# A causal pool mixer whose window sums are taken by VectorE, against one whose running means are matrix products on TensorE

## The chip, the cores and the metric

One core of one Trainium2 chip runs the whole kernel: TensorE (PE, with its weight loads as PEld), VectorE (DVE), ScalarE (ACT), GpSimd (POOL) and SyncE (SP), which issues most of the loads. The metric is the device time of one launch, in microseconds, as the median over runs.

## The reference

Two transformer blocks over 256 tokens of width 1024. The first block has two layers; the change is in layer 0, whose mixer is this:

```python
def pool_mixer(u, pool_w, pool_scale):                 # u: 256 tokens x 768 = 4 groups of 192
    ...
    win = jnp.array(POOL_WINDOWS, jnp.int32)           # 2, 4, 8, 16
    lo = jnp.maximum(t + 1 - win[None, :], 0)
    cnt = jnp.minimum(t + 1, win[None, :])
    window_sum = csum[:, 1:] - csum[:, lo, ...]
    d = window_sum / cnt - uf                          # mean of the last w tokens, less the own one
    mixed = jnp.einsum('bsgc,gcd->bsgd', d, pool_w)    # one 192 x 192 product for each group
    return mixed.reshape(B, S, MAIN_WIDTH) * pool_scale

proj = rmsnorm(h, norm_mix[l]) @ w_in[l]
main, mq = proj[..., :MAIN_WIDTH], proj[..., MAIN_WIDTH:]
main_out = pool_mixer(main, pool_w[l], pool_scale[l])
mem_out = memory_attention(mqh, mk, mv)                # 4 heads over 256 memory rows
h = h + jnp.concatenate([main_out, mem_out], -1) @ w_out[l]
```

The mean runs over tokens and `pool_w` over channels, so the two may be taken in either order.

## The kernel before

All 256 tokens stay on the chip (two tiles `tt` of 128). Weights stream in as units of 256 rows x 512 columns; ACT casts each to `wh`, DVE makes the rest `wl = raw - wh`, and every large product is three fp32r products (`xh*wh`, `xh*wl`, `xl*wh`) on PE. PE's program is one fixed order of instructions; in the first stage it is written by hand, later a planner (`Line`) lays tasks by rank and estimated lateness, and a scheduler fixes each engine's order. Each engine runs its own queue in order and waits on semaphores.

The part that matters is the first 110 us:

- **In projection, transposed.** Six banks `ups` of channels x tokens (128 x 256) are summed from `w_in` and the raw input; `queries` does the 256 columns of the memory queries into `qs`. The norm of each token, `x_r`, comes later than the products, so it is put in afterwards: `dg` is a diagonal of `x_r`, the products of `ones` with `dg` (L807) spread it over all partitions, `rb` is their copy, and `u = ups * rb` (L817) is the mixer's input.
- **Memory keys and values, layer 0 and 1.** `rows` sums `mem @ w_mem_kv[0]` into `accs1`: 48 fp32r products of 512 columns. `memkv1` follows with 48 more, then the 96 of `out0`.
- **`pool_mix`.** For each of four window levels DVE (tiles 0 to 4) and POOL (tile 5) add shifted copies into `win`, correct the first tokens by `short`, and write `mean - u` back into `u` (L923 to L929). A group of 192 channels lies across two of the six tiles, so the eight `PIECES` are 128 or 64 partitions high. Then 16 fp32 products `mm<-u,pw` with 256 columns follow, whose contraction is 128 or 64 channels and whose output 128 or 64 partitions. ACT (L944) and DVE (L945) split each result to `xh`, `xl` of `mts`, which `out0` reads.
- **`mem_attention`.** Scores `acc<-mkT,mqT` (contraction 64), softmax on DVE and ACT (tile `me`), four transposes `mm<-ident,me` for each half, values `mm<-eT,mv` (64 output partitions).
- **`out0`.** `mixer_out` with no cuts: every row tile is one sum over all eight k-tiles and waits for both `pooled` and `recalled[tt]`.

An fp32 product is run as two passes (two rows in the trace); an fp32r product is one, and so is a transpose.

Of the kernel before, what the change touches and what calls it, by code (L numbers as in the profile page):

```python
# [41 lines left out]
def kernel(  # L42
# [149 lines left out]
    def col(i, n=1):  # L192
        return cols[:, i:i + n]
# [94 lines left out]
    def plan_rows(key, w, cuts):  # L288
        for k0, k1 in zip((0,) + cuts, cuts + (KT,)):
            for c in range(2):  # L290
                planned((key, k0, c), [(w, c * 512, 512)], k1 - k0, k0 * P)
# [2 lines left out]
        planned(("in0", c), [(w_in[0], c * 512, 512)])  # L294
    planned("memkv0", [(w_mem_kv[0], 0, 512)], g=G_MEM + 0)
    planned("memkv1", [(w_mem_kv[1], 0, 512)], g=G_MEM + 8)
    plan_rows("out0", w_out[0], ())
    plan_mlp("mlp0", 8, lambda b: [(w_up[0], b * 512, 512)], w_down[0], 4)
    planned("kv", [(w_kv, 0, 512)], g=G_KV)
    plan_cols("in1", w_in[1], G_MIX + 8)  # L300
# [377 lines left out]

    act.open("mix0", 7)

    u = act.tile([P, 6, S], F32, tag="u", name="u")
    mq = [act.tile([P, 256], F32, tag="mq", name="mq", bufs=TT) for _ in range(TT)]


# [4 lines left out]
    short = act.tile([P, 4, 16], F32, tag="short", name="short")  # L689

    def pool_short():
        cnt = act.tile([P, 16], F32, tag="cnt", name="cnt")
        G.iota(cnt, [[1, 16]], base=1, channel_multiplier=0, allow_small_or_imprecise_dtypes=True)
        V.reciprocal(cnt, cnt)
        for g, w in enumerate(WIN):
            V.tensor_scalar(short[:, g, :], cnt, float(w), None, op0=ALU.mult)

    def run(steps):
        for _ in steps:
# [24 lines left out]
    with tc.manual_schedule(engines={ET.DVE, ET.Activation, ET.Pool, ET.PE}):  # L724

        x_raw, m_raw = raw_T(), raw_T()

        warm = mm_bank()
        for _ in range(12):
            PE.matmul(warm[:, :P], ones, ones, start=True, stop=True)  # L730

        def units_of(i, **a):
            key, w = plan[i][:2]
            ready[key] = []
            units = load_units(*w, **a)

            def more():
                ready[key] += next(units)
                return ready[key][-KU:], len(ready[key]) - KU

            return more

        def columns_T(ps, xs, w, k, c0):

            for i, (wh, wl) in enumerate(w):
                xh, xl = ktiles(xs)[k + i]
                c = slice(c0, c0 + P)
                for j, (a, b) in enumerate(((wh, xh), (wh, xl), (wl, xh))):
                    mm(ps, a[:, c], b, k + i + j == 0, k + i == KT - 1 and j == 2)

        def rows(accs, xs, w, k):
            for tt in range(TT):
                run(lin(accs[tt], ktiles(xs, tt)[k:k + KU], w, k == 0, k + KU == KT))


        load_T(x_raw, xT, 0, 2)
        nc.scalar.dma_start(gcols, gains)
        load_T(x_raw, xT, 2, 2, nc.scalar)

        A.activation(early, ones[:, :1], AF.Copy, scale=2.0)  # L760
        ups = [acc_bank()[:, :S] for _ in range(4)]
        more = units_of(0, apart=KU + 1)
        for k in range(0, KT, KU):
            if k >= 4:
# [7 lines left out]
        pool_short()  # L772
# [12 lines left out]
        dg = act.tile([P, TT, P], F32, tag="dg", name="dg")  # L785
        nx = [Norm(h[tt]) for tt in range(TT)]
        for tt in range(TT):
            for c in range(2):
                nx[tt].add(c)
            x_r[tt] = nx[tt].rstd()  # L790
            V.tensor_scalar(dg[:, tt, :], ident, x_r[tt], None, op0=ALU.mult)
        split_raw(m_raw, mem_set, 0, 4)
        qs = mm_bank().rearrange("p (t c) -> p t c", t=TT)
        rb = act.tile([P, S], F32, tag="rb", name="rb")
        m = [act.tile([P, D], F32, tag="raw_T", name="mem", bufs=4) for _ in range(TT)]
        more = units_of(2)

        def queries(tt):
            run(lin(qs[:, tt, :], ktiles(xs0, tt), [(wh[:, 256:], wl[:, 256:]) for wh, wl in ws]))

        def mem_rows(tt):
            mem_r[tt] = row_norm(m[tt])

        queries(0)
        ps = mm_bank()[:, :S]
        for tt in range(TT):
            PE.matmul(ps[:, tok(tt)], ones, dg[:, tt, :], start=True, stop=True)  # L807
        nc.gpsimd.dma_start(pw, pool_w[0].rearrange("g a d -> (g a) d").rearrange("(j p) d -> p j d", p=P))

        split_raw(m_raw, mem_set, 4, 4)  # L810
        w0 = more()
        tc.keep_in_program_order(nc.sync.dma_start(m[0], mem[0, tok(0), :]))
        mem_rows(0)
        A.copy(rb, ps)
        queries(1)
        for i in range(6):
            V.tensor_tensor(u[:, i, :], ups[i], rb, ALU.mult)  # L817
        w1 = more()
        accs1 = [acc_bank() for _ in range(2)]
        rows(accs1, mem_set, *w0)  # L820
        tc.keep_in_program_order(nc.sync.dma_start(m[1], mem[0, tok(1), :]))
        mem_rows(1)
        rows(accs1, mem_set, *w1)
        for tt in range(TT):
            A.activation(mq[tt], qs[:, tt, :], AF.Copy, scale=x_r[tt])
        for _ in range(2):
            rows(accs1, mem_set, *more())
        for e in mem_there:
            e.at()
    W("memkv0")  # L830
# [80 lines left out]

    def pool_mix(xs, done):

        a, b = (act.tile([P, 6, S], F32, tag="win", name="win", bufs=2) for _ in range(2))
        prev = u
        for lev, (k0, s) in enumerate(((0, a), (1, b), (3, a), (4, b))):
            n = 1 << lev
            for eng, t0, t1 in ((V, k0, 5), (G, 5, 6)):  # L920
                if t0 < t1:
                    o = slice(t0, t1)
                    eng.tensor_copy(s[:, o, :n], prev[:, o, :n])  # L923
                    eng.tensor_tensor(s[:, o, n:], prev[:, o, n:], prev[:, o, :S - n], ALU.add)  # L924
            for k, p0, p1, g in PIECES:
                if g == lev:
                    r, w = s[p0:p1, k, :], WIN[g]
                    V.tensor_tensor(r[:, :w], r[:, :w], short[p0:p1, g, :w], ALU.mult)  # L928
                    V.scalar_tensor_tensor(u[p0:p1, k, :], r, 1.0 / w, u[p0:p1, k, :], op0=ALU.mult, op1=ALU.subtract)  # L929
            prev = s  # L930
        for k0 in range(0, 6, 2):
            yield 6.0 if k0 == 0 else 0
            ps = mm_bank().rearrange("p (k t) -> p k t", t=S)
            for k in (k0, k0 + 1):
                for t, q0, q1, g in PIECES:
                    if t != k:
                        continue
                    d0 = k * P + q0 - g * 192
                    src = [(t2, r0, r1) for t2, r0, r1, g2 in PIECES if g2 == g]
                    for i, (t2, r0, r1) in enumerate(src):  # L940
                        mm(ps[q0:q1, k - k0, :], pw[r0:r1, t2, d0:d0 + q1 - q0], u[r0:r1, t2, :],
                           i == 0, i == len(src) - 1)
                xh, xl = (t[:, k, :] for t in xs)
                A.activation(xh, ps[:, k - k0, :], AF.Copy, scale=col(V_PSCALE + k))  # L944
                V.scalar_tensor_tensor(xl, ps[:, k - k0, :], col(V_PSCALE + k), xh.bitcast(F32),  # L945
                                       op0=ALU.mult, op1=ALU.subtract)
        done.at(1.5)

    mem_kv = {0: add_mem_kv(0, 0, 6.0, accs1)}


# [6 lines left out]
    mts = xset()  # L958
# [3 lines left out]
    line.add(4, pool_mix(mts, pooled))  # L962
# [628 lines left out]
```

## Time and profile before

| | |
|---|---|
| median of 3 runs | 1034.71 us (1034.3 to 1035.31) |
| the profiled execution | 1037.36 us, its span 1035.4 us |
| PE busy | 1027.9 us (99% of the span) |
| DVE, ACT, POOL busy | 638.5, 562.8, 97.7 us |
| mean granted clock of TensorE | 0.997 |

PE is busy almost the whole span, but a row of PE holds about 0.17 us of pipeline beyond the start of the next, so short waits don't show as idle time: the spacing of starts is what to read. The span is that of the profiled execution; 1.96 us of its time lie around it.

### The profile page before, as it was taken

The page shows a single profiled execution, that of the slowest core. Times are in us where ns is not written, and L with a number is a line of the kernel's source. Part 1 is how long each engine was busy: PE and PEld are TensorE (multiplying, and loading weights), DVE is VectorE, ACT ScalarE, POOL GpSimd, SP SyncE. Part 2 cuts the span into 40 slices and gives each one's busy share as a digit, 9 for nine tenths or more (in the row PEclk, how much of TensorE's full clock was granted, in tenths as well). Part 3 has the DMA queues.
Part 4 walks back from the last instruction along what each step waited for, and adds up shares of the span by engine and source line. Part 5 has one row for each costly group of instructions (what it writes and reads, how often), then busy time and mean ns, then how long its engine had stood idle before and what let it go on. Part 6 is the DMA issues. An engine that isn't in the chain of part 4 may idle for free.

```text
span 1035.4 us, 18410 instructions
## 1 busy us (share of the span) xinstructions
PE 1027.9 (99%) x7352; PEld 907.0 (88%) x7352; DVE 638.5 (62%) x1002; ACT 562.8 (54%) x902; POOL 97.7 (9%) x143
## 2 busy tenths in 40 slices
PE   9999999999999999999999999999999999999998
PEld 8858999998876788899988988888999988999997
DVE  6976665555678766564576569847635766464552
ACT  7855554454678654444465445758644556344351
POOL 1515000000143000000001003330000000000000
PEclk9989999999999999999999999999999999999999
DMA  9854556556642259666557554344355566565741
GB/s 341 273 161 138 187 179 211 183 167 208 195 163 82 66 183 322 202 193 211 168 183 246 182 164 157 118 135 149 116 201 186 165 197 209 164 211 163 234 145 41
DMA packets 107765, 186.40 MB, mean 180 GB/s; under 512 B 6808, under 2 KB 31648, under 8 KB 107680
## 3 DMA queue, kind: packets, MB, share of 16 engines
q1 hardware_dynamic: 106160, 180.13, 53.2%
q0 software_dynamic: 1104, 4.80, 1.4%
q8 instruction: 57, 0.93, 0.4%
q10 hardware_dynamic: 416, 0.30, 0.1%
q14 instruction: 28, 0.23, 0.1%
HBM read 182.58 MB, written 2.63 MB: 179 GB/s over the span
## 4 chain that ended last, share of the span: by engine, by line
PE 97%; DVE 1%; DMA 0%; issue 0%; ACT 0%; SPq 0%; ACTq 0%
PE acc L152 61%; PE mm L152 34%; PE mm L159 3%; DMA raw<-in_w_in_dram 0%; DVE wl L243 0%; DVE u L929 0%; DVE wl L248 0%; DVE win L924 0%; DVE win L928 0%; DVE hs L424 0%; ACT wh L242 0%; ACT wh L247 0%; ACT mv L847 0%; SPq L232 0%; PE mm L807 0%
## 5 line engine op out<-in xcount | busy, mean ns | idle before, releaser
L243 DVE TENSOR_TENSOR wl<-raw,wh 128x1024 fp32r<-128x1024 f32 (+1 forms) x316 | 378.1, 1219 | 173.3 <-ACT wh L242 168.0
L242 ACT CAST wh<-raw 128x1024 fp32r<-128x1024 f32 (+1 forms) x316 | 322.5, 1045 | 169.0 <-PE acc L152 100.0
L152 PE MATMUL mm<-xh,wh 128*128 128x256 f32 x752 | 208.3, 277 | 0.0
L152 PE MATMUL mm<-xl,wh 128*128 128x256 f32 x752 | 207.9, 276 | 0.0
L152 PE MATMUL mm<-xh,wl 128*128 128x256 f32 x752 | 207.8, 276 | 0.0
L152 PEld LDWEIGHTS mm<-xh,wh 128*128 128x128 f32 x752 | 141.2, 188 | 1.4 <-issue 0.4
L152 PEld LDWEIGHTS mm<-xl,wh 128*128 128x128 f32 x752 | 141.3, 188 | 1.0
L152 PEld LDWEIGHTS mm<-xh,wl 128*128 128x128 f32 x752 | 141.3, 188 | 0.0
L152 PE MATMUL acc<-wh,xh 128*128 128x512 f32 x336 | 138.6, 412 | 0.0
L152 PE MATMUL acc<-wh,yl 128*128 128x512 f32 x342 | 134.7, 394 | 0.0
L152 PE MATMUL acc<-wl,yh 128*128 128x512 f32 x342 | 134.0, 392 | 0.0
L152 PE MATMUL acc<-wh,yh 128*128 128x512 f32 x342 | 133.4, 390 | 0.0
L152 PE MATMUL acc<-wh,xl 128*128 128x512 f32 x336 | 132.7, 395 | 0.0
L152 PE MATMUL acc<-wl,xh 128*128 128x512 f32 x336 | 132.5, 394 | 0.0
L152 PE MATMUL acc<-xh,wh 128*128 128x256 f32 x416 | 117.0, 281 | 0.5 <-ACT wh L242 0.5
L152 PE MATMUL acc<-xh,wl 128*128 128x256 f32 x416 | 116.5, 280 | 0.4 <-DVE wl L243 0.4
L152 PE MATMUL acc<-xl,wh 128*128 128x256 f32 x416 | 116.3, 279 | 0.0
L152 PEld LDWEIGHTS acc<-xh,wl 128*128 128x128 f32 x416 | 78.8, 189 | 0.9 <-DVE wl L243 0.9
L152 PEld LDWEIGHTS acc<-xh,wh 128*128 128x128 f32 x416 | 78.6, 189 | 0.9 <-ACT wh L242 0.7
L152 PEld LDWEIGHTS acc<-xl,wh 128*128 128x128 f32 x416 | 78.1, 188 | 0.0
L152 PEld LDWEIGHTS acc<-wh,xh 128*128 128x128 f32 x336 | 63.4, 189 | 15.2 <-issue 3.2
L152 PEld LDWEIGHTS acc<-wl,yh 128*128 128x128 f32 x342 | 64.2, 188 | 13.7
(239 smaller groups left out, 1278.7 us busy)
## 6 DMA issues: line engine op xcount, KB each, us to landing
raw<-in_w_in_dram SPq DMA_DIRECT2D x86, 512.0 KB, 4.9
raw<-in_w_up_dram SPq DMA_DIRECT2D x64, 512.0 KB, 4.7
raw<-in_w_down_dram SPq DMA_DIRECT2D x64, 512.0 KB, 4.8
raw<-in_w_out_dram SPq DMA_DIRECT2D x24, 512.0 KB, 4.7
raw<-in_w_ffn_gate_dram SPq DMA_DIRECT2D x44, 256.0 KB, 4.3
raw<-in_w_ffn_up_dram SPq DMA_DIRECT2D x44, 256.0 KB, 4.6
raw<-in_w_ffn_down_dram SPq DMA_DIRECT2D x22, 512.0 KB, 5.1
raw<-in_w_mem_kv_dram SPq DMA_DIRECT2D x8, 512.0 KB, 9.2
```

The costliest lines, as they stand in the source:

```text
L152: PE.matmul(out_, lhsT, rhs, start=start, stop=stop)
L159: PE.transpose(out_, in_, ident)
L242: A.copy(wh[:, ks, :], raw[:, ks, :])
L243: V.tensor_sub(wl[:, ks, :], raw[:, ks, :], wh[:, ks, :].bitcast(F32))
```

## The change

The mixer's order is turned round. `pool_groups(tt)` first multiplies each group's raw channels by `pool_w` (tokens as output partitions, 192 columns), and ACT scales by the token's norm on the way out, to `yp`: so `dg`, `rb` and the products with `ones` are gone, and `u` is a plain copy of `ups`. `pool_mix` then takes the mean less the own token as products with `means`, constant matrices over tokens, made once at the start by POOL and DVE: for each piece 128 columns of tile 0, 128 of tile 1, and 16 that carry tile 0's last tokens into tile 1. The window sums on DVE and POOL are gone. `pool_groups` and `pool_mix` are written into the hand-ordered stage between `rows`, and `out0` is cut into k-tiles 0 to 5 and 6 to 7, so that the first part waits for `pooled` alone.

```diff
-    plan_rows("out0", w_out[0], ())
+    plan_rows("out0", w_out[0], (6,))
...
+    FIRST, OWN = P + 16, P
+    means = act.tile([P, 4, FIRST + OWN], F32, tag="means", name="means")
+    def pool_windows():
...
+        for g, w in enumerate(WIN):
+            G.memset(means[:, g, :], 1.0 / w)
+            V.tensor_scalar(means[:, g, :16], cnt, float(w), None, op0=ALU.min)
+            V.reciprocal(means[:, g, :16], means[:, g, :16])
+        for g, w in enumerate(WIN):
+            for m in (means[:, g, :FIRST], means[:, g, FIRST:]):
+                n = m.shape[1]
+                G.affine_select(m, m, [[1, n]], ALU.is_ge, 0.0, base=0, channel_multiplier=-1)
+                G.affine_select(m, m, [[-1, n]], ALU.is_ge, 0.0, base=w - 1, channel_multiplier=1)
+    def pool_less_own():
+        for m in (means[:, :, :P], means[:, :, FIRST:]):
+            V.tensor_tensor(m, m, ident[:, None, :].to_broadcast([P, 4, P]), ALU.subtract)
...
-            V.tensor_scalar(dg[:, tt, :], ident, x_r[tt], None, op0=ALU.mult)
-            PE.matmul(ps[:, tok(tt)], ones, dg[:, tt, :], start=True, stop=True)
-        A.copy(rb, ps)
-            V.tensor_tensor(u[:, i, :], ups[i], rb, ALU.mult)
+            V.tensor_copy(u[:, i, :], ups[i])
...
+        def pool_groups(tt):
+            for g0 in range(2):
+                ps = mm_bank()[:, :384].rearrange("p (g d) -> p g d", g=2)
+                for g in (g0, g0 + 2):
+                    src = [(t, r0, r1) for t, r0, r1, g2 in PIECES if g2 == g]
+                    for i, (t, r0, r1) in enumerate(src):
+                        mm(ps[:, g // 2, :], u[r0:r1, t, tok(tt)], pw[r0:r1, t, :], i == 0, i == len(src) - 1)
+                A.activation(yp[:, tt]..., ps, AF.Copy, scale=x_r[tt])
+        def pool_mix(xs, k0):
...
+                    mm(o[:, :P], yp[:, 0, f], means[:, g, :P])
+                    mm(o[:, P:], yp[:, 1, f], means[:, g, FIRST:], True, False)
+                    mm(o[:, P:FIRST], yp[:, 0, f], means[:, g, P:FIRST], False, True)
...
-    t = mixer_out("out0", mts, (), [[[pooled, recalled[tt]]] for tt in range(TT)])
+    t = mixer_out("out0", mts, (6,), [[[pooled], [recalled[tt]]] for tt in range(TT)])
```

The order on PE where the mixer's products stand, before: they come as `mm<-u,pw` after all of `memkv1`, among the scores of the memory attention (`mkT`, `mqT`).

```order
L159 MATMUL mm<-ident,ks 128x128 x4
L152 MATMUL mm<-u,pw 128x256 x4
L152 MATMUL acc<-mkT_571,mqT 128x256 x4
L152 MATMUL mm<-u,pw 64x256 x4
L152 MATMUL acc<-mkT_571,mqT 128x256 x2
L152 MATMUL acc<-wh,xh 128x512
...
L152 MATMUL mm<-u,pw 64x256 x4
...
L152 MATMUL mm<-u,pw 128x256 x2
L152 MATMUL acc<-mkT_571,mqT 128x256
L152 MATMUL mm<-u,pw 128x256 x2
```

Now the 16 group products (`mm<-pw,u`, in two lots of 8) stand between the first three units of `memkv0`, and the products with `means` among those of `memkv1`; here the second lot of the latter, k-tiles 3 and 4.

```order
L152 MATMUL acc<-wh,xh 128x512
L152 MATMUL mm<-means,yp 128x128 x2
L152 MATMUL mm<-means,yp 128x16
L152 MATMUL mm<-means,yp 64x128 x2
L152 MATMUL mm<-means,yp 64x16
L152 MATMUL mm<-means,yp 64x128 x2
L152 MATMUL mm<-means,yp 64x16
L159 MATMUL mm<-ident,mq 128x128 x4
L152 MATMUL acc<-wl,xh 128x512
```

So what waited for DVE's window sums late in the stage now waits for ACT's `yp` early in it. The memory attention stands alone afterwards on PE, after `memkv1`, with the first part of `out0` around it; the last two score products are split off behind four products of `memkv1`.

```order
L152 MATMUL acc<-mkT_654,mqT 128x256 x6
L152 MATMUL acc<-wh,xl 128x512
L152 MATMUL acc<-wh,xh 128x512
L152 MATMUL acc<-wl,xh 128x512
L152 MATMUL acc<-wh,xl 128x512
L152 MATMUL acc<-mkT_654,mqT 128x256 x2
L159 MATMUL mm<-ident,me 128x128 x4
L159 MATMUL mm<-ident,ks 128x128 x2
```

Before, its scores and its values were spread over four places each; now the scores stand in two places and the sixteen value products in one.

## Rows read from the trace of the kernel before

**Rows 1.** The page: busy time, clock in 40 slices, chain by engine.

```profile
PE 1027.9 (99%) x7352; PEld 907.0 (88%) x7352; DVE 638.5 (62%) x1002; ACT 562.8 (54%) x902; POOL 97.7 (9%) x143
...
PEclk9989999999999999999999999999999999999999
...
PE 97%; DVE 1%; DMA 0%; issue 0%; ACT 0%; SPq 0%; ACTq 0%
```

**Rows 2.** Stretches: length, each engine's busy time (instructions), granted clock, DMA.

```profile
49.00:55.50 6.50, 5.36 (x27) 2.38 (x25) 6.38 (x17) 3.40 (x7) 1.91 (x1) 1.00 0.31 101
55.50:62.20 6.70, 6.70 (x17) 3.40 (x17) 3.79 (x9) 0.47 (x1) 1.62 (x2) 0.50 0.71 237
```

**Rows 3.** The chain that ended last, in order of time: start, length, work.

```profile
51.27 1.14 DVE wl L243
...
52.63 1.24 DVE wl L243
...
83.12 4.15 PE acc L152 x18
```

**Rows 4.** Timeline of PE, 49 to 67 us: start, length, passes [idle before].

```profile
49.14 1.86 PE L152 MATMUL mm<-u,pw 128*128 128x256 f32 x8
50.93 1.13 PE L152 MATMUL acc<-mkT,mqT 64*128 64x256 f32 x8
52.00 1.22 PE L152 MATMUL mm<-u,pw 128*64 128x256 f32 x4
54.36 1.22 PE L152 MATMUL mm<-u,pw 64*64 64x256 f32 x4 [1.14 <-DVE u L929]
55.51 2.07 PE L152 MATMUL acc<-mkT,mqT 64*128 64x256 f32 x4
...
59.94 2.88 PE L152 MATMUL mm<-u,pw 128*64 128x256 f32 x8
...
63.78 1.00 PE L152 MATMUL mm<-u,pw 128*128 128x256 f32 x3
...
66.07 0.60 PE L159 MATMUL mm<-ident,me 128*128 128x128 f32 x4
```

**Rows 5.** Timeline of PE elsewhere: fp32 passes of few columns.

```profile
27.12 0.61 PE L807 MATMUL mm<-dg,ones 128*128 128x128 f32 x4
...
655.35 1.10 PE L152 MATMUL mm<-fQ,fK 128*32 128x32 f32 x32
...
676.82 2.17 PE L152 MATMUL mm<-hv,AT 128*128 128x128 f32 x18
678.83 0.39 PE L152 MATMUL mm<-hv,AX 128*128 128x128 f32 x2
```

**Rows 6.** Timeline of PE: one of four runs of value products.

```profile
73.93 1.09 PE L152 MATMUL mm<-eT,mv 128*64 128x128 f32 x14
```

**Rows 7.** The load of `pw`: its issue on POOL, and its landing.

```profile
23.52 1.07 POOL L808 DMA_DIRECT2D pw<-in_pool_w_dram  x1
...
DMA to landing us min/median/max: 7.9/7.9/7.9
```

**Rows 8.** Timeline of DVE and ACT: softmax of the memory attention.

```profile
57.40 1.28 DVE L887 TENSOR_REDUCE ms<-acc 128x2 f32<-128x512 f32 x2
...
63.23 0.56 ACT L892 ACTIVATE me<-acc,ms,mr 128x256 f32<-128x256 f32 x1
```

**Rows 9.** Timeline of POOL and DVE: a select, and DVE beside POOL.

```profile
1.19 0.28 POOL L200 TENSOR_SCALAR_AFFINE_SELECT ident<-ones 128x128 f32<-128x128 f32 x1
...
7.07 0.69 DVE L243 TENSOR_TENSOR wl<-raw,wh 128x512 fp32r<-128x512 f32 x1 [0.97 <-ACT wh L242]
...
26.49 1.41 DVE L248 SCALAR_TENSOR_TENSOR wl<-raw,gcols,wh 128x512 fp32r<-128x512 f32 x2
...
38.16 3.27 DVE L248 SCALAR_TENSOR_TENSOR wl<-raw,gcols,wh 128x512 fp32r<-128x512 f32 x4
...
38.85 1.47 POOL L345 TENSOR_TENSOR mr<-hs,mhalf 128x4 f32<-128x4 f32 x1
```

More of the change, by code (lines that the diff above doesn't have):

```diff
@@ L681 @@
     u = act.tile([P, 6, S], F32, tag="u", name="u")
+    yp = act.tile([P, TT, 768], F32, tag="yp", name="yp")
     mq = [act.tile([P, 256], F32, tag="mq", name="mq", bufs=TT) for _ in range(TT)]
@@ L687 @@
               (3, 0, P, 2), (4, 0, 64, 2), (4, 64, P, 3), (5, 0, P, 3))
-    short = act.tile([P, 4, 16], F32, tag="short", name="short")
-    def pool_short():
+    FIRST, OWN = P + 16, P
+    means = act.tile([P, 4, FIRST + OWN], F32, tag="means", name="means")
+    def pool_windows():
         cnt = act.tile([P, 16], F32, tag="cnt", name="cnt")
         G.iota(cnt, [[1, 16]], base=1, channel_multiplier=0, allow_small_or_imprecise_dtypes=True)
-        V.reciprocal(cnt, cnt)
         for g, w in enumerate(WIN):
-            V.tensor_scalar(short[:, g, :], cnt, float(w), None, op0=ALU.mult)
+            G.memset(means[:, g, :], 1.0 / w)
[9 more added lines that the diff above has]
+            V.tensor_tensor(m, m, ident[:, None, :].to_broadcast([P, 4, P]), ALU.subtract)
     def run(steps):
@@ L726 @@
         x_raw, m_raw = raw_T(), raw_T()
+        pool_windows()
         warm = mm_bank()
@@ L771 @@
         more = units_of(1)
-        pool_short()
         ws = []
@@ L783 @@
             load_T(m_raw, memT, k, 4)
-        dg = act.tile([P, TT, P], F32, tag="dg", name="dg")
+        for i in range(6):
+            V.tensor_copy(u[:, i, :], ups[i])
+        pool_less_own()
         nx = [Norm(h[tt]) for tt in range(TT)]
@@ L790 @@
             x_r[tt] = nx[tt].rstd()
-            V.tensor_scalar(dg[:, tt, :], ident, x_r[tt], None, op0=ALU.mult)
+        nc.gpsimd.dma_start(pw, pool_w[0].rearrange("g a d -> (g a) d").rearrange("(j p) d -> p j d", p=P))
         split_raw(m_raw, mem_set, 0, 4)
         qs = mm_bank().rearrange("p (t c) -> p t c", t=TT)
-        rb = act.tile([P, S], F32, tag="rb", name="rb")
         m = [act.tile([P, D], F32, tag="raw_T", name="mem", bufs=4) for _ in range(TT)]
@@ L802, in mem_rows @@
             mem_r[tt] = row_norm(m[tt])
+        def pool_groups(tt):
[5 more added lines that the diff above has]
+                        mm(ps[:, g // 2, :], u[r0:r1, t, tok(tt)], pw[r0:r1, t, :], i == 0, i == len(src) - 1)
+                A.activation(yp[:, tt].rearrange("p (a b d) -> p b a d", a=2, b=2)[:, g0], ps, AF.Copy, scale=x_r[tt])
@@ new lines, in pool_mix @@
+        def pool_mix(xs, k0):
+            ps = mm_bank().rearrange("p (k t) -> p k t", t=S)
+            for k in (k0, k0 + 1):
+                for t, q0, q1, g in PIECES:
+                    if t != k:
+                        continue
+                    o, f = ps[q0:q1, k - k0, :], slice(k * P + q0, k * P + q1)
+                    mm(o[:, :P], yp[:, 0, f], means[:, g, :P])
+                    mm(o[:, P:], yp[:, 1, f], means[:, g, FIRST:], True, False)
+                    mm(o[:, P:FIRST], yp[:, 0, f], means[:, g, P:FIRST], False, True)
+                xh, xl = (t[:, k, :] for t in xs)
+                A.activation(xh, ps[:, k - k0, :], AF.Copy, scale=col(V_PSCALE + k))
+                V.scalar_tensor_tensor(xl, ps[:, k - k0, :], col(V_PSCALE + k), xh.bitcast(F32),
+                                       op0=ALU.mult, op1=ALU.subtract)
@@ L804 @@
         queries(0)
-        ps = mm_bank()[:, :S]
-        for tt in range(TT):
-            PE.matmul(ps[:, tok(tt)], ones, dg[:, tt, :], start=True, stop=True)
-        nc.gpsimd.dma_start(pw, pool_w[0].rearrange("g a d -> (g a) d").rearrange("(j p) d -> p j d", p=P))
+        queries(1)
         split_raw(m_raw, mem_set, 4, 4)
-        w0 = more()
+        w = more()
         tc.keep_in_program_order(nc.sync.dma_start(m[0], mem[0, tok(0), :]))
         mem_rows(0)
-        A.copy(rb, ps)
-        queries(1)
@@ L816 @@
-        for i in range(6):
-            V.tensor_tensor(u[:, i, :], ups[i], rb, ALU.mult)
-        w1 = more()
         accs1 = [acc_bank() for _ in range(2)]
-        rows(accs1, mem_set, *w0)
+        rows(accs1, mem_set, *w)
+        w = more()
         tc.keep_in_program_order(nc.sync.dma_start(m[1], mem[0, tok(1), :]))
-        mem_rows(1)
-        rows(accs1, mem_set, *w1)
         for tt in range(TT):
             A.activation(mq[tt], qs[:, tt, :], AF.Copy, scale=x_r[tt])
-        for _ in range(2):
-            rows(accs1, mem_set, *more())
+        pool_groups(0)
@@ L828 @@
+        mem_rows(1)
+        rows(accs1, mem_set, *w)
+        w = more()
+        pool_groups(1)
+        rows(accs1, mem_set, *w)
+        rows(accs1, mem_set, *more())
+        mts = xset()
+        for k0 in range(0, 6, 2):
+            pool_mix(mts, k0)
         for e in mem_there:
@@ L910, in mem_attention @@
         done.at(3.0)
[L914 to L947, printed above, removed]
     mem_kv = {0: add_mem_kv(0, 0, 6.0, accs1)}
@@ L956 @@
         V.scalar_tensor_tensor(qk_gain[:, i:i + 1], col(a), s, col(b), op0=ALU.mult, op1=ALU.mult)
-    mts = xset()
     mem_kv[1] = add_mem_kv(1, 14, 9.0)
@@ L961 @@
     q_there.at()
-    line.add(4, pool_mix(mts, pooled))
+    pooled.at(2.0)
     for tt in range(TT):
```

## The prediction

> **What bounds the kernel now.** I read the page first: PE is busy for 1027.9 of 1035.4 us and holds 97% of the chain that ended last [rows 1]. So a change here is worth what it adds to PE's own work, plus the few places where PE waits or runs slowly. The clock line has one slice of 40 with an 8, the third, 51.8 to 77.7 us [rows 1]. The table of stretches says what that is: from 55.5 to 62.2 us the granted clock is 0.50, the lower of the two levels (1.2 against 2.4 GHz), and beside it, from 49.0 to 55.5, it is 1.00 [rows 2]. The chain of waits leaves PE just ahead of this: DVE makes two `wl` (51.27, 52.63) and only then the last piece of `u`, and PE's timeline shows the wait for it, 1.14 us before 54.36 [rows 3, 4]. DVE is busy for 6.38 of the 6.50 us there [rows 2]. So the pool mixer costs PE three things: its products, a wait of 1.14 us on DVE, and a slow stretch that begins 1.1 us after that wait.
>
> **What the change removes.** The wait: 1.14 us [rows 4]. The slow stretch: 6.70 us at half the clock, so 3.35 us, if it doesn't come back; what PE did before it fell is the wait and a run of half-height products [rows 2, 4]. Together 4.5 us.
>
> The 32 passes `u,pw`, by starts: 49.14 to 50.93 is 1.79; the four from 52.00, 1.22 less about 0.17 of pipeline, 1.05; 54.36 to 55.51, 1.15; the eight from 59.94 took 2.88, most at half clock (until about 62.3), at full clock 1.6; 63.78 to 66.07 holds the last eight, and two score passes beside them, about 2.2 [rows 4]. Sum 7.8 us. The four passes with `ones`: 18 passes of that size took 676.82 to 678.83, or 0.112 us each, so 0.45 us [rows 5]. Removed in all 4.5 + 7.8 + 0.45 = 12.75 us.
>
> DVE's sums over `win` are off the list: they cost PE the 1.14 us and no more.
>
> **What it adds on PE.** *Group products*: per token tile eight products of 192 columns, 16 passes. Such a pass stands between 0.112 (128 columns) and the 256 columns of the first eight `u,pw`. Those eight lasted 1.79 us, with four of them (contraction 64, on the two halves of the array) side by side: six slots, some 0.22 each, and the rest, about 0.4, is two changes between full and half height, 0.2 each [rows 4, 5]. Midway I take 0.166 a pass. Contraction 128: 4 products x 2 x 0.166 = 1.33; contraction 64: four products, of which two adjacent ones run side by side, 3 x 2 x 0.166 = 1.0; six changes x 0.2 = 1.2. That is 3.5 us, and twice 7.0 us.
>
> *Products with `means`*: eight pieces, each four passes of 128 columns and two of 16. A 16-column pass behind a fresh load of 128 weight columns is nowhere in the trace. Above it stands the 128-column pass, 0.112; below, the passes of 32 columns with 32 weight columns, 32 in 1.10 us, 0.033 each [rows 5]. It loads as many weights as the first, so I take 0.11. Four full-height pieces: 4 x 6 x 0.112 = 2.7. Four half-height ones load 64 columns, so 4 x (4 x 0.112 + 2 x 0.06) = 2.3, less 0.4 where the second of two neighbours starts on the other half before the first has ended. Their four changes: 0.6. Sum 5.2 us.
>
> The Trainium skill (TensorE: Matmul & The Clock Gate, "LDWEIGHTS (loading the stationary operand)") puts a weight load at its columns over 1.2 GHz, whatever the contraction, so 107 ns for 128. By that rule, an estimate from the page, the 16-column passes cost as much as those of 128 and the 5.2 us stand; by the lower row they would be 4.5.
>
> *Order*: the sixteen value products, before in four runs, become one. A run of 14 passes, mostly in pairs, took 1.09 us, 0.75 of it passes [rows 6], so three runs fewer give back about 3 x 0.4 = 1.2 us. The scores lose 0.3 of it: two products of the second token tile fall on one half of the array and can't pair. Net 0.9 us off.
>
> So PE's work: + 7.0 + 5.2 - 7.8 - 0.45 - 0.9 = + 3.05 us.
>
> **New waits.** *Scores.* The last two score products write a bank that the first two filled, so they wait until its maxima and its exponentials have been taken: 1.28 us (two maxima), some 0.2 for the small products, two exponentials of 0.56, 0.1 of signalling, 2.7 us [rows 8]. PE has meanwhile two score products (0.85), four of 512 columns (4.15 / 18 = 0.23 each, 0.92 [rows 3]) and two changes (0.4): 2.2. So it waits 0.5 us. Queued behind are the transposes of `me`, and DVE and ACT feed them no later than PE then comes.
> *Start.* POOL now makes 16 selects of about 0.28 us from 2.5 us on; some ten fall on DVE's first `xl` and `wl`, which PE awaits [rows 9]. DVE beside POOL is slower: two `wl` alone took 1.41 us, four beside POOL 3.27 [rows 9], 0.45 more. Between nothing and ten selects in full (2.8 us, which the stream from 8 us on partly absorbs) I take 0.3.
>
> **Priced at nothing.** The eight small DVE instructions that make `means` stand ahead of the first `xl`, while the first loads are on their way; at 7.07 DVE still waits 0.97 us for ACT [rows 9]. In the stream's way they would cost at most 0.28 us each, the select's time on eight times the columns. Plain copies `u` cost what the products with `rb` did, and move before `wl`, where `queries` (48 passes) cover them. `pw` was issued at 23.52 and landed 7.9 us later, at 31.4 [rows 7]; it was needed at 49.14 and is now needed near 32.7 us (12 products of 0.23 behind the start of `rows` at 29.96, which is 0.45 earlier). One `x` tile now loads ahead of the last three `w_in` units, and they ahead of the norms, so POOL's issue slips by about 0.9 us: cover 0.4 us, and beyond it each 0.1 us late is 0.1 us of PE. ACT's four `yp` stand in front of `wh` units that PE wants only a unit later. The second residual of `out0` (four more DVE additions) lies under 12 products each time.
>
> **The sum.** - 4.5 + 3.05 + 0.5 + 0.3 = - 0.65, call it - 0.7 us. Against the profiled 1037.36 us (span 1035.4 and 1.96 around it) that is 1036.7. The runs shown have a median of 1034.71, 2.65 us below the profiled execution, so the forecast is 1034.0 us.
>
> **The rivals.**
> *Slower: the clock gives nothing back.* Either the timed runs hold no slow stretch (they are 2.65 us faster than the profiled one, and it cost 3.35), or the new wait at the scores brings it on again, as the wait of 1.14 us did at 54.36 [rows 2, 4]. For it: the new wait too stands among half-height passes. Against it: the new wait is half as long, and the three runs lie within 1.0 us of each other, so all of them or none hold the slow stretch, as the profiled one does. The price is 3.35 us: 1037.4 us. It decides from 1.4 us at 0.50 (0.7 lost, no gain left); 5.5 us make it slower by 0.2%.
> *Faster: the small products are cheaper.* If changes cost 0.1 rather than 0.2 (16 of them, 1.6 us) and 16-column passes 0.033 (0.7 us), and the wait at the scores vanishes because maxima and exponentials start before the fourth product is done (0.5): 2.5 to 2.8 us less, 1031.3 us. For it: 32 small passes in 1.10 us [rows 5]; against: all `u,pw` runs show the larger change.
> *DVE is held up at the start.* The Trainium skill (SBUF — State Buffer, "Who interferes with whom") says that a DVE instruction with two SBUF inputs and a GpSimd one that reads SBUF exclude each other for the whole instruction. The trace agrees as far as the 3.27 us go. As a mechanism of this kernel: DVE's `wl` at 7.07, the last that PE waits for at the start, comes behind selects of 0.28 us [rows 9]; four such meetings are 1.1 us in place of 0.3, so 1034.8 us.
>
> **How the numbers follow.** Forecast (within 1.5 us of 1034.0) 0.48; small products cheap 0.24; the clock 0.20; the start 0.08. 0.2% is 2.07 us, about what a measurement of this kernel can tell from none. Faster: the second case and a twelfth of the first, 0.28. Slower: the clock, and a little of the first and last, 0.22. Same: 0.50. The range runs from 1031.3, most of the cheap case, to 1037.4; the likeliest case's own is 1032.5 to 1035.5.
>
> **What would show it.** Right: in the profile after, no idle on PE between 45 and 65 us; 1.00 in every stretch up to 90 us; 32 passes `pw,u` in about 7.0 us and the 48 passes `means,yp` in about 5.2; a wait of about 0.5 us before the last score products; the first `wl` up to 0.3 us later. It would be wrong if 0.50 appears in a stretch again, if PE waits for `pw`, for `yp` or for `wh` in `memkv0`, or if passes at a change cost half of what I took.

## The result: slower by 0.7%

The change takes 1043.2 us (median of 6 runs, 1039.23 to 1044.86), and the kernel before 1035.01 us beside it: a ratio of 1.0071 (95% interval 1.0050 to 1.0093). The forecast was 1034.0 us, and its range ended at 1037.4. The profiled execution of the change took 1044.86 us, its span 1043.2 us.

The page of the change, the lines that answer to [rows 1]:

```profile
PE 1033.2 (99%) x7396; PEld 914.4 (88%) x7396; DVE 635.4 (61%) x985; ACT 564.4 (54%) x905; POOL 98.7 (9%) x155
...
PEclk9899999999999999999999999999999999999999
...
PE 95%; DMA 3%; ACT 1%; issue 0%; DVE 0%; POOL 0%; ACTq 0%; DVEq 0%
```

PE still holds the chain, but loads (DMA) have 3% of it where they had none (`pw` alone 1%), and ACT has 1%. One slice of the clock line holds an 8, as before, but it is now the second. The table of stretches of the change (length, busy time and instructions of PE, PEld, DVE, ACT and POOL, granted clock, DMA share, GB/s) answers to [rows 2]:

```profile
25.00:36.10 11.10, 9.21 (x63) 7.73 (x62) 6.70 (x10) 5.87 (x12) 3.81 (x4) 1.00 1.04 376
36.10:43.00 6.90, 6.90 (x20) 4.82 (x18) 1.20 (x2) 3.60 (x8) 0.86 (x2) 0.51 0.07 25
...
55.50:62.20 6.70, 6.70 (x53) 6.02 (x50) 6.34 (x12) 6.25 (x12) 3.75 (x5) 1.00 0.66 223
62.20:73.60 11.40, 9.55 (x51) 7.24 (x49) 10.00 (x17) 7.62 (x16) 2.31 (x3) 1.00 0.91 280
73.60:80.60 7.00, 7.00 (x23) 5.48 (x24) 3.56 (x14) 4.23 (x15) 0.00 (x0) 0.51 0.17 64
```

The slow stretch of before, at 55.5 us, is gone (1.00). Two others have come, from 36.1 and from 73.6 us, each at half clock. PE's timeline of the change (start, length, passes, idle before) shows what stands ahead of each; it answers to [rows 4]. A row pass is one product of 512 columns (`acc<-wh,xh` and its like), a lot the eight group products of one token tile, which are 16 passes:

```profile
34.27 5.05 PE L152 MATMUL mm<-pw,u 128*128 128x192 f32 x16 [1.89 <-DMA pw<-in_pool_w_dram]
...
39.55 0.63 PE L152 MATMUL acc<-wl,xh 128*128 128x512 f32 x1
39.97 0.63 PE L152 MATMUL acc<-wh,xl 128*128 128x512 f32 x1
...
43.68 3.62 PE L152 MATMUL mm<-pw,u 128*128 128x192 f32 x16
...
68.54 1.99 PE L152 MATMUL acc<-mkT,mqT 64*128 64x256 f32 x12
...
73.52 1.93 PE L152 MATMUL acc<-mkT,mqT 64*128 64x256 f32 x4 [1.85 <-ACT me L933]
```

PE waits 1.89 us for the load of `pw`, and the clock falls 1.9 us later; it waits 1.85 us for the exponentials `me` ahead of the last score products, and the clock falls 0.2 us after that. The first lot of group products takes 5.05 us against 3.62 for the second, and the row passes behind it step by 0.42 instead of 0.23 us. So 3.74 us of waits stand where 1.14 stood, and each slow stretch, some 6.9 us at half the clock, costs about 3.4 us.

Where the first wait comes from: POOL's timeline, with the landing of `pw`, answers to [rows 7], and SP's issues show one load of `h` ahead of the last three of `w_in`.

```profile
24.92 1.07 POOL L807 DMA_DIRECT2D pw<-in_pool_w_dram  x1
...
DMA to landing us min/median/max: 9.2/9.2/9.2
...
6.55 0.60 SPq L795 DMA_DIRECT2D h<-in_x_dram  x1
7.92 5.30 SPq L232 DMA_DIRECT2D raw<-in_w_in_dram  x3
```

SP's issues in the kernel before had the last five loads of `w_in` in a row, and both loads of `h` behind them:

```profile
5.22 8.02 SPq L232 DMA_DIRECT2D raw<-in_w_in_dram  x5
13.29 0.93 SPq L780 DMA_DIRECT2D h<-in_x_dram  x2
```

The load of `pw` is issued 1.40 us later than before and takes 1.3 us longer, so it lands at 34.1 us; PE is there at 34.27 - 1.89 = 32.4. Where the second comes from: DVE's and ACT's timelines around the scores, which answer to [rows 8]:

```profile
68.12 2.78 DVE L243 TENSOR_TENSOR wl<-raw,wh 128x1024 fp32r<-128x1024 f32 x2
70.83 1.27 DVE L928 TENSOR_REDUCE ms<-acc 128x2 f32<-128x512 f32 x2
72.03 0.27 DVE L929 TENSOR_TENSOR ms<-ms,mr 128x2 f32<-128x2 f32 x2
...
72.26 0.56 ACT L933 ACTIVATE me<-acc,ms,mr 128x256 f32<-128x256 f32 x1 [2.95 <-DVE ms L929]
72.82 0.56 ACT L933 ACTIVATE me<-acc,ms,mr 128x256 f32<-128x256 f32 x1
```

The first maximum starts as the second `wl` ends: in DVE's order two copies of later weights stand ahead of it. ACT, which takes the exponentials, sits idle for 2.95 us until DVE's maxima are there.

### The profile page after: what moved, and what is told of

Same layout as the page of the kernel before. It is cut to its first block, busy times and chain, and to the rows that moved or that the text cites. A ratio compares the mean times of both kernels' runs of the same rounds, so it can differ in the third digit from the quotient of the medians.

```text
span 1043.2 us, 18508 instructions
## 1 busy us (share of the span) xinstructions
PE 1033.2 (99%) x7396; PEld 914.4 (88%) x7396; DVE 635.4 (61%) x985; ACT 564.4 (54%) x905; POOL 98.7 (9%) x155
## 4 chain that ended last, share of the span: by engine, by line
PE 95%; DMA 3%; ACT 1%; issue 0%; DVE 0%; POOL 0%; ACTq 0%; DVEq 0%
PE acc L152 59%; PE mm L152 33%; PE mm L159 3%; DMA raw<-in_w_in_dram 1%; DMA pw<-in_pool_w_dram 1%; DMA raw_T<-in_xT_dram 0%; ACT wh L242 0%; ACT xn L395 0%; DVE wl L243 0%; ACT me L933 0%; DVE ms L928 0%; POOL st L345 0%; ACT mv L888 0%; ACTq L773 0%; DVE h L1539 0%
## 5 line engine op out<-in xcount | busy, mean ns | idle before, releaser
L152 PEld LDWEIGHTS acc<-wh,xl 128*128 128x128 f32 x336 | 63.8, 190 | 14.4 <-issue 0.3
```

The source lines that it names most:

```text
L152: PE.matmul(out_, lhsT, rhs, start=start, stop=stop)
```

## The experiments

Theory: the two waits, with the lower clock behind each, are the whole loss, and they come from the late load and from the scores. Rivals: the products themselves cost more than was reckoned; the lower clock belongs to their half-height passes and not to waits; the cut of the output rows is to blame. Every ratio is to the kernel before on the same chip. Waits are those of PE in the profiled run from 0.25 us up; the ones ahead of 9 us (1.05 us for `ones`, the others under 0.7) and near 614 to 626 us (0.5 to 1.4 us, in all but one of the kernels) are left out. The clock is that of the profiled run, with 0.5 for each stretch at half clock (the last 2 us of the span left out). The last column counts the timed runs whose mean granted clock over the whole span was 0.999 or 1.000: a stretch of 6.83 us at half clock takes 0.003 off this mean.

| run | median us | ratio (95%) | waits of PE | granted clock | runs at 0.999 or 1.000 |
|---|---|---|---|---|---|
| the change | 1043.2 | 1.0071 (1.0050 to 1.0093) | 1.89, 1.85 | 0.5 twice | 0 of 6 |
| groups_later | 1034.62 | 0.9995 (0.9986 to 1.0003) | 0.31 | 1.00 | 11 of 11 |
| scores_later | 1043.6 | 1.0074 (1.0059 to 1.0090) | 1.68, 1.59, 0.26 | 0.5 twice | 0 of 6 |
| both_later | 1039.1 | 1.0038 (1.0026 to 1.0050) | 1.66, 0.26 | 1.00 | 2 of 9 |
| cut_only | 1034.25 | 0.9990 (0.9982 to 0.9999) | 1.07 | 1.00 | 11 of 11 |
| fewer_changes | 1032.95 | 0.9985 (0.9977 to 0.9994) | 0.31 | 1.00 | 12 of 12 |
| pw_early | 1038.94 | 1.0042 (1.0028 to 1.0055) | 0.50, 0.41, 1.85 | 1.00 | 2 of 6 |
| load_late | 1041.9 | 1.0069 (1.0055 to 1.0084) | 3.56, 0.31 | 0.5 once | 0 of 4 |
| before_later | 1034.54 | 0.9995 (0.9987 to 1.0004) | 1.07, 1.28 | 1.00 | 12 of 12 |
| h_behind | 1037.61 | 1.0038 (1.0026 to 1.0051) | 1.85 | 0.5 once | 0 of 10 |
| no_cut | 1037.32 | 1.0035 (1.0021 to 1.0048) | 1.71, 0.68 | 0.5 once | 7 of 11 |
| fewer_no_cut | 1034.03 | 0.9993 (0.9984 to 1.0002) | 0.35, 0.31 | 1.00 | 11 of 11 |
| fewer_h_behind | 1033.09 | 0.9983 (0.9975 to 0.9992) | 0.31 | 1.00 | 11 of 11 |
| scores_later_layer0 | 1036.11 | 1.0012 (1.0001 to 1.0024) | 1.65 | 0.5 once | 9 of 12 |
| both_causes | 1034.36 | 1.0001 (0.9990 to 1.0012) | none | 1.00 | 10 of 11 |
| fewer_scores | 1033.68 | 0.9988 (0.9979 to 0.9997) | none | 1.00 | 11 of 11 |

**The first lot one unit later (groups_later).**

```diff
+        mem_rows(1)
+        rows(accs1, mem_set, *w)
+        w = more()
         pool_groups(0)
-        mem_rows(1)
         rows(accs1, mem_set, *w)
         w = more()
         pool_groups(1)
         rows(accs1, mem_set, *w)
-        rows(accs1, mem_set, *more())
```

> The change, with one edit: each lot of group products stands one unit of the memory's rows later, so 24 row passes (5.5 us) instead of 12 lie ahead of the first lot. If the late load of the products' matrix is the cause of the first loss, PE's 1.89 us wait at 34.27 goes, and with it the stretch at clock 0.50 from 36.15 (half of 6.83 us, 3.4 us): about 5.3 us less than the change, 1038 us. If the lower clock belongs to the half-height group products themselves and not to the wait, only the wait goes and a 0.50 stretch follows the first lot as before: about 1041.3 us. If the time is given back later (the scores then wait longer, since the filling rows were used up sooner), about 1043 us and a longer wait at the scores. The order at the scores moves a little too (11 row passes instead of 4 ahead of the last two score products), so the wait of 1.85 us there may shrink as well, down to 1033 us if it goes with its stretch.

It went down by 8.6 us, to the time of the kernel before. PE's timeline of this run, and a table of stretches:

```profile
34.67 3.62 PE L152 MATMUL mm<-pw,u 128*128 128x192 f32 x16
...
47.10 0.73 PE L152 MATMUL mm<-means,yp 128*128 128x128 f32 x6
47.69 0.48 PE L152 MATMUL acc<-wh,xh 128*128 128x512 f32 x1
48.01 0.39 PE L152 MATMUL acc<-wl,xh 128*128 128x512 f32 x1
...
66.19 1.13 PE L152 MATMUL acc<-mkT,mqT 64*128 64x256 f32 x4 [0.31 <-ACT me L934]
...
35.00:100.00 65.00, 64.69 (x358) 51.37 (x358) 46.54 (x90) 46.38 (x97) 26.38 (x27) 1.00 0.53 167
```

The same products, the half-height ones among them (contraction 64), run here at full clock: the lower clock isn't theirs. In this execution `pw` landed early, at 31.97 us: at the change's place, 12 x 0.23 us ahead of 34.67, PE would hardly have waited either. In both_later, fewer_changes, fewer_no_cut and fewer_scores it landed at 33.8 to 34.4, later than that place and still 0.8 to 1.0 us ahead of PE. The scores gain too, since 11 row passes instead of 4 now lie ahead of the last two: 7 x 0.23 = 1.6 us more cover leaves 0.25 of the 1.85, near the 0.31 that is seen.

**The second scores later (scores_later; scores_later_layer0; both_later).**

```diff
         yield kv_there
+        if l == 0 and tt:
+            yield 7.0
...
-        yield 3.2
+        yield 5.5 if l == 0 else 3.2
```

This is scores_later_layer0. The two runs made first had the edit without `l == 0`, so in both layers.

> The change, with one edit: the second half's score products are planned 7 us after the first half's, and the turns of the exponentials 5.5 instead of 3.2 us after the scores. If the 1.85 us wait of PE at the last two score products (for the exponentials that free their bank) and the 0.50 stretch behind it are the second loss, both go: 5.3 us less than the change, 1038 us, while the wait at 34.27 and its stretch stay. If the stretch at 73.70 has another cause than the wait: 1041.3 us. If the wait only moves to the turns of the exponentials or the value products: about 1043 us, with a wait of over 1 us named there.

> The change with both edits. If the two waits and the stretches behind them are the whole of what went wrong, 10.5 us less than the change: 1032.5 us, which is 2.5 us under the kernel before (whose own wait of 1.14 us and stretch cost 4.5 us, while the change's products cost some 3 us more on PE). If the products themselves cost more than the 3 us of the prediction, it stays above that: 1035 us or more without any wait. If the waits move elsewhere, 1038 us and over.

By their times both came out by their last case. The wait at the scores of layer 0 went, but it didn't move to the turns or the values there: a new one stood at 327.55 us (at 323.24 in both_later), in layer 1, whose attention is made by the same function. PE waits there for `pj`, a projection of that layer, which ACT copies out. PE's timeline of scores_later:

```profile
327.55 0.44 PE L159 MATMUL mm<-ident,pj 128*128 128x128 f32 x2 [1.59 <-ACT pj L662]
```

both_later's profile is at full clock, but seven of its nine timed runs are at 0.997 or 0.998. The edit had reached further than was meant, so it was made again for layer 0 alone:

> The change with the edit at the scores in layer 0 alone; the run before it delayed the scores and turns of layer 1 as well, since both layers share the function. If PE's 1.85 us at the last score products and the clock behind it are the second loss, and the wait of 1.59 us at 327.55 came from the delay in layer 1, that wait goes too, and the wait at 34 us with its 0.50 stretch is the only large one left: from 1043.2 less 1.85 and 3.4, 1038 us. If the later scores only move the wait (to the turns or the value products of layer 0), or the wait at 327 us stays, 1040 to 1043 us.

The wait in layer 1 is gone. What is left in the profiled run (1038.1 us) is the load and the one stretch behind it:

```profile
33.84 5.07 PE L152 MATMUL mm<-pw,u 128*128 128x192 f32 x16 [1.65 <-DMA pw<-in_pool_w_dram]
...
35.70:42.50 6.80, 6.80 (x19) 4.78 (x16) 1.11 (x2) 3.60 (x8) 0.86 (x2) 0.50 0.12 45
```

The median is 7.1 us under the change, more than the 5.3 expected. The granted clocks tell why: nine of the 12 runs are at 0.999 or 1.000 (1034.09 to 1036.54 us), and only the other three, at 0.996 or 0.997, are as slow as the profiled one (1038.10 to 1039.85). The fastest are as fast as both_causes below, so they can hold little of the wait either.

**The load earlier or later (pw_early, load_late).** The issue on POOL stands behind the selects in the one (10.30 us), and behind the norm of the memory's first half in the other (30.90 us; with the groups one unit later).

> The change, with one edit: the load of the products' matrix is issued on POOL right behind the constants' selects (about 10.4 us) instead of behind the norms (24.92), and the order on PE is the change's. If the late load is the cause of the first loss, PE's wait at 34.27 and the 0.50 stretch behind it go: 5.3 us less, 1038 us, with the score wait and its stretch still there. The 0.59 MB now stand among the loads of the first weights (some 390 GB/s there, so 1.5 us of the queues): if these are what PE is about to wait for, up to 1.5 us comes back as waits among the first 25 us: 1039.5 us. If the order of the products and not the load makes the 0.50 stretch: 1041.3 us.

> As the run with the groups one unit later, with the load of the products' matrix issued later on POOL, behind the norm of the memory's first half (about 31 instead of 24.9 us), so that it lands near 37 to 40 us, 2 to 5 us after PE comes to the first lot at 34.7. If such a wait draws the 0.50 stretch behind it, the time is 1034.6 plus the wait plus 3.4: 1040 to 1043 us. If the stretches have another cause, 1034.6 plus the wait alone: 1036.6 to 1039.6 us, at clock 1.0 throughout.

load_late came by its first case. pw_early lies between its first two: the wait for `pw` goes, and part of the gain comes back as waits ahead of 25 us. PE's timelines, two rows of pw_early and one of load_late, and a stretch of load_late:

```profile
20.65 0.39 PE L152 MATMUL mm<-xh,wl 128*128 128x256 f32 x1 [0.50 <-DVE wl L243]
22.70 0.38 PE L152 MATMUL mm<-xh,wl 128*128 128x256 f32 x1 [0.41 <-DVE wl L243]
```

```profile
39.30 5.97 PE L152 MATMUL mm<-pw,u 128*128 128x192 f32 x16 [3.56 <-DMA pw<-in_pool_w_dram]
...
40.00:46.90 6.90, 6.90 (x19) 4.34 (x19) 0.36 (x1) 2.17 (x4) 0.00 (x0) 0.51 0.01 2
```

The early load takes the wait away and puts 0.91 us of others among the first weights: the last three loads of `w_in` land 1.3 to 1.7 us later than in the change. The late load, issued at 30.90 and landed 8.3 us later, brings this loss back to the version that was free of it, and a larger one: a wait of 3.56 us and half clock behind it, 7.3 us by the medians.

**SP's order (h_behind).** The loads of `h`, `columns` and `memT` are kept in program order, which puts both `h` loads behind `w_in` again; on every other engine the order is that of the change.

```diff
-            nc.sync.dma_start(h[tt], x[0, tok(tt), :])
+            tc.keep_in_program_order(nc.sync.dma_start(h[tt], x[0, tok(tt), :]))
```

> The change with SP's order of loads as in the kernel before: both loads of h behind the last of w_in, where the change has one of them ahead of the last three. Nothing else moves on any engine. If that load is what makes the products' matrix late (the last w_in units, then their copies on ACT, then the norms, then the issue on POOL: 24.92 instead of 23.52, and 9.2 instead of 7.9 us to landing), the issue comes back to about 23.5 and the landing to 31.5 to 32.7, when PE is there at 32.4: the wait of 1.89 us shrinks to 0 to 0.3 us and the 0.50 stretch goes: 1038 to 1039.6 us, with the score wait still there. If the norms are late for another reason (POOL's or DVE's constants), nothing changes: 1043 us.

The issue comes at 23.36, the landing 8.0 us later at 31.4, and PE, there at 31.96, doesn't wait for it. So that one load of `h` is what made `pw` late. The score wait stays, 1.85 us, as in the change.

```profile
23.36 1.07 POOL L807 DMA_DIRECT2D pw<-in_pool_w_dram  x1
...
DMA to landing us min/median/max: 8.0/8.0/8.0
...
68.02 1.13 PE L152 MATMUL acc<-mkT,mqT 64*128 64x256 f32 x4 [1.85 <-ACT me L933]
...
69.90:73.40 3.50, 3.50 (x13) 2.80 (x12) 2.17 (x10) 2.29 (x9) 0.00 (x0) 0.51 0.00 0
```

**Both causes (both_causes):** h_behind and scores_later_layer0 together, every product where the change has it.

> The change with its two losses taken away each at its own place, and the products left where the change has them: SP's loads in the order of the kernel before, and the scores of the second half later in layer 0. PE's own work, worked out as span less waits and half of the slow stretches, was 1031.1 to 1031.5 us in the versions so far; with it and waits of 0.5 to 1 us, 1033.5 to 1034.5 us by the runs' median, the same as the kernel before. If a third loss hides behind the two, 1036 us or more.

1034.36 us, 8.8 us less than the change and the same as before. The stretch that holds both places has no idle time on PE and full clock:

```profile
25.00:100.00 75.00, 75.00 (x423) 59.97 (x422) 54.62 (x99) 54.56 (x116) 25.27 (x31) 1.00 0.59 196
```

No third loss hides behind the two: the profiled spans of the change and of this run differ by 10.9 us, and the waits (3.74) with half of the two slow stretches (6.8) make 10.6 of it.

**The cut (cut_only, no_cut).** The cut `(6,)` put into the kernel before, and taken out of the change.

> The kernel before, with only the output rows of layer 0 in two parts (the cut after six row blocks). If the cut is harmless, as the prediction took it, within 1 us of before: 1034 to 1036 us, with the wait at 54.36 for the running means and its 0.50 stretch still there. If the cut costs (its rows hold two more banks while the scores are worked on, and the residual is added twice), 1036 to 1039 us, with a wait for a bank at the scores. If it fills waits that before leaves open, 1030 to 1033 us.

> The change without the cut of the output rows. If the cut has a part in the score wait (the copies of its weights stand on DVE ahead of the maxima, its rows hold banks), the 1.85 us wait and its stretch shrink: 1038 us. If the cut's rows fill time that would else be waited out (before it, the rows needed both halves of the mixer), the waits at the scores grow by 1 to 3 us: 1044 to 1046 us. If it does neither, 1043 us with the same two waits.

Alone it gains about 0.1% (at most 0.2%, by the interval). Its time is that of its first case, but the wait for `u` that this case kept isn't in its profile: PE waits 1.07 us for `ks` instead, at full clock. In the change the cut has a part in the score wait: without it one `wl` stands ahead of the first maximum and 9 row passes instead of 4 ahead of the last scores, and PE doesn't wait there. Which of the two does it, the run doesn't tell apart. DVE's timeline of no_cut:

```profile
66.41 1.23 DVE L243 TENSOR_TENSOR wl<-raw,wh 128x1024 fp32r<-128x1024 f32 x1
67.55 1.28 DVE L928 TENSOR_REDUCE ms<-acc 128x2 f32<-128x512 f32 x2
```

**The kernel before without its wait (before_later):** `yield 6.0` of `pool_mix` is 9.0.

> The kernel before, with its first group product planned 9 instead of 6 us after the mixer starts, so that more rows lie ahead of it. If PE's wait of 1.14 us at 54.36 for the running means is all that holds the kernel before, it goes: 1033.5 us, 1.1 us under the version of the change without its waits (1034.6), which would be the price of the change's products on PE. If the means are late for the later products too, the wait only moves: 1034.7 us.

The wait for `u` is gone, but 1.07 us for `ks` and 1.28 us ahead of a later product have come, and the time is the same, so the wait's own price wasn't got at in this way.

**Fewer changes of height (fewer_changes, fewer_no_cut, fewer_h_behind, fewer_scores).** On groups_later, both banks of a token tile are opened at once and the eight products follow in the order of `PIECES`, which puts the half-height ones of the two halves side by side:

```diff
-            for g0 in range(2):
-                ps = mm_bank()[:, :384].rearrange("p (g d) -> p g d", g=2)
+            pss = [mm_bank()[:, :384].rearrange("p (g d) -> p g d", g=2) for _ in range(2)]
+            for i, (t, r0, r1, g) in enumerate(PIECES):
+                mm(pss[g % 2][:, g // 2, :], u[r0:r1, t, tok(tt)], pw[r0:r1, t, :], i % 2 == 0, i % 2 == 1)
```

> As the run with the groups one unit later, and the eight products of a lot in another order: the four of half height in two pairs, side by side in the upper and lower rows, so that a lot changes between full and half height four times instead of six, and both pairs run abreast instead of one. If a change of height costs the 0.2 us of the prediction (0.25 us by the profile of that run, against 0.16 for a pass of the same height), a lot of 3.62 us becomes some 2.7 us: 1.8 us less, 1032.8 us. If the passes cost by their columns and not by the changes, no more than 0.3 us: 1034.4 us.

> The best version so far (groups one unit later, fewer changes of height: 1032.95) without the cut. By what the cut alone did to the kernel before (1034.25 against 1034.72) 0.4 us more: 1033.4 us. If the cut's rows are needed as filling behind the earlier products, 1034 to 1036 us with a wait behind the scores. If the cut costs by its second addition to the residual, 1032 us.

> The best version so far with SP's loads in the order of the kernel before. If the h load ahead of w_in costs PE only through the products' matrix, which this version no longer waits for, no difference: 1032.9 us. If it also holds up the first weights (the waits of 0.2 to 0.35 us in the first 8 us lie ahead of it, and later units had up to 1.5 us of slack), up to 0.3 us less.

> The best version (groups one unit later, fewer changes of height) with the second half's scores planned 2 us later in layer 0, so that four score products stand in a row, twelve row passes follow, and then the other four, in pairs: the wait of 0.31 us there goes and two lone products pair: 0.3 to 0.8 us less, 1032.3 us. If the turns of the exponentials, which now follow 0.2 us behind the second scores, have to wait instead: 1033 us or more.

A lot takes 2.91 instead of 3.62 us, so 1.4 us of the 1.8 expected for the two, and by the medians the version is 1.7 us faster than both groups_later and before. PE's timeline of fewer_changes:

```profile
34.79 2.91 PE L152 MATMUL mm<-pw,u 128*128 128x192 f32 x16
```

The cut may be worth some 0.8 us in it (0.9993 against 0.9985 without and with it), but the two intervals overlap, and the profile of fewer_no_cut has a wait of 0.35 us at 21.77 that isn't the cut's. The `h` load and the rest of the score wait are worth nothing more: 1033.09 and 1033.68 lie inside the runs of fewer_changes (1032.23 to 1034.55). For fewer_scores 0.3 to 0.8 us less had been expected; the wait went, and the time didn't fall.

## Why the prediction was wrong

**The step that failed first: the cover of `pw`, "0.4 us", priced at nothing.** The cause was seen (an `h` load ahead of the last three `w_in` units, and these ahead of the norms), but the slip was put at 0.9 us and the flight left at the 7.9 us of [rows 7]. In the profiled run the slip is 1.40 and the flight 9.2 us, and PE comes at 32.4 instead of 32.7: together the 0.4 us of cover turn into 1.89 us of wait. h_behind and load_late show it from both sides. Over all profiles the slip was fairly judged and the flight was not. With that `h` load early (nine profiles) the issue comes at 24.2 to 25.3 us, with both behind (six) at 23.4 to 24.1; the flight takes 9.1 to 9.4 us in the first kind, but 7.7 in groups_later, and 7.9 to 8.0 in the second, but 9.3 in before_later. What makes the flight long or short stays open. By the prediction's own rule, that each 0.1 us beyond the cover is 0.1 us of PE, a cover of 0.4 us on an estimate made of two others, smaller than the spread of the flights, had to go into the sum as a risk and not as nothing.

**The second: the new wait at the scores, 0.5 us.** The chain was right (maxima, small products, two exponentials, the bank: 2.7 us from 70.83 to 73.52) and PE's 2.2 us of cover too: from about 69.5 to 71.67 in the trace. But the maxima were taken to start as the fourth product ends. They start 1.3 us later, behind two `wl`, and 0.5 + 1.3 is the 1.85 measured. In the kernel before two `wl` stood ahead of `u` in the same way [rows 3]. That DVE's queue is the reason is read from the rows of the change and of no_cut; an experiment that moves these `wl` alone wasn't made.

**The third: 3.35 us given back by the clock.** The wait of before and the slow stretch behind it in [rows 2] are gone, as forecast, but the median held nothing of the stretch. Each run's mean granted clock is on record; the profiled execution, with its stretch, is at 0.997. Of the 110 runs of the kernel before beside these experiments only 7 are as low (0.996 or 0.997, 1036.29 to 1037.79 us) and 17 are at 0.998; the other 86 are at 0.999 or 1.000, with a median of 1034.4. cut_only and before_later keep waits of 1.07 and 1.28 us, and all of their 23 runs are at 0.999 or 1.000. The prediction had this among its rivals ("Either the timed runs hold no slow stretch (they are 2.65 us faster than the profiled one, and it cost 3.35)") and set it aside because three runs agreed with each other; their distance from the profiled execution was the better evidence. With this term left out the forecast would have been 1037.4 us, the end of the range.

**The first rival was the case, twice over.** Its mechanism, that a new wait brings on 0.50 again, came at the scores and at `pw`, and the signs that the prediction named for being wrong (0.50 in a stretch again, PE waiting for `pw`) are the two that came. It was priced with one stretch and no wait for `pw`; two waits of 3.7 us and two stretches make the rest.

**PE's own work, + 3.05 us, was too much by 1 to 2.** From the profiled runs at clock 1.00 throughout, span less all waits of 0.25 us and more behind the first load: with the change's products both_causes 1032.3 - 1.2 = 1031.1 and groups_later 1032.3 - 0.8 = 1031.5, with those of before cut_only 1032.2 - 2.6 = 1029.6 and before_later 1032.5 - 2.4 = 1030.1. So the products cost 1 to 2 us net, an estimate from four profiles. The lots were right: by starts the two take 6.6 to 6.7 us, against 7.0. A full-height piece with `means` was right as well: six passes from 47.10, the row behind them at 47.69 and 0.09 late itself, 0.68 us, against 6 x 0.112. The Trainium skill (TensorE: Matmul & The Clock Gate, "LDWEIGHTS (loading the stationary operand)") puts a weight load at its columns over 1.2 GHz, so 107 ns for 128. Six of them are 0.64 us, an estimate from that page, and the piece of 0.68 us agrees with it. The half-height pieces cost less than was reckoned: all 48 passes take 4.4 us by starts in groups_later, against 5.2. What was taken off was too much in turn: the old `u,pw` passes at full clock take 7.0 to 7.3 us (cut_only, before_later) instead of 7.8. By these figures the products alone add some 3.5 us, so the order must give back 1.5 to 2.5 us instead of 0.9; this is the remainder of the sum and wasn't measured by itself. The small-products rival was wrong on the price of a change, which is 0.2 us as the prediction had it (see the last section), and right on this side of the forecast.

**DVE at the start: 0.3 us, and the third rival.** Not seen: PE's waits there are 0.35 and 0.22 us against 0.23, 0.55 and 0.22 before, and the last of them ends at 7.95 against 7.82 us.

## What to carry to other kernels

A transfer whose need moves forward has to be followed back to what issues it, and each link's slip added, the spread of its flight too (7.7 to 9.8 us for this one load over all runs here); a cover smaller than the spread of that sum must be priced as a wait. A short wait on PE can cost nearly twice its length more by the clock behind it (1.85 and 3.4 us here), so filling work belongs ahead of the first use of anything new: here 12 row passes moved in front of the products were worth 8.6 us, since both waits all but went. And a slow stretch in one profiled execution is credited only if the timed runs are as slow as that execution and their granted clocks as low.

## What the runs showed of the hardware

The lower clock isn't certain after a wait. The same wait of 1.85 us at the scores was followed by half clock over some 7.0 us in the profile of the change, over some 3.5 us in that of h_behind, and by none in that of pw_early, whose stretch there, read from its table, is at 1.00:

```profile
60.00:90.00 30.00, 28.15 (x165) 22.29 (x164) 18.67 (x40) 18.39 (x47) 14.29 (x19) 1.00 0.38 125
```

The spread of h_behind's runs goes with their clocks: the six at 1037.29 to 1037.67 us are at 0.998, the slowest, 1043.71, at 0.993. Waits of 0.31 us were followed by none in the five profiles that have them there, and of the 67 runs of the six versions with no wait above 0.35 us in their row of the table 66 are at 0.999 or 1.000.

A lot of products of mixed height costs by its order: the same eight products take 3.62 us with six changes of height and one half-height pair side by side, and 2.91 with four changes and two pairs. The starts of the single passes in groups_later and fewer_changes tell the two apart: a pass steps by 0.16 us behind one of its own height, and the two passes behind a change step by 0.25 and 0.27, so a change costs 0.2 us. Of the 0.71 us saved, two changes are 0.4 and the second pair the other 0.3.
